# Weight sums of the first channel tile: from the vector engine to adding DMAs and a detour through DRAM

## The chip, the core and the metric

The kernel runs on one core of one Trainium2 chip. The metric is the device time of one execution in microseconds (us). A core has five engines that work side by side: TensorE (PE: matmuls, with weight loads as PEld), VectorE (DVE), ScalarE (ACT), GpSimd (POOL) and SyncE (SP, whose queue issues most DMAs here). Each works through its own list of instructions in order and waits on semaphores for the others.

## What is computed

One decoder layer with 1024 tokens, width 1024 and float32 data: a mixing sub-layer (attention heads and retention heads), an output projection, a layer norm, a GEGLU channel mixer with a causal convolution of width 3, a second layer norm.

```python
mix = jnp.concatenate([fox, ret], axis=-1) @ w_out[l]
x = layer_norm(ALPHA * x + g1 * mix, ln1_g[l], ln1_b[l])
h = x * (1.0 + sc2) + sh2
u = causal_depthwise_conv(h @ w_up[l], conv_w[l], conv_b[l])
a, bv = jnp.split(u, 2, axis=-1)
y = (jax.nn.gelu(a, approximate=False) * bv) @ w_down[l]
x = layer_norm(ALPHA * x + g2 * y, ln2_g[l], ln2_b[l])
```

The change lies in the weights of `h @ w_up`.

## The kernel before

**Stages.** Up to 224 us: retention and the input projections; then the values; 271 to 499: the attention heads, 8 heads of 8 query blocks each; about 476 to 579: the output projection, eight blocks of 128 tokens, each followed by its layer norm and its transposes; 579 to 1002: the up projection, 22 channel tiles of 128 (`NFF`); then the down projection.

**Three matmuls for one.** Every float32 operand is kept as two parts, a high part (rounded by ScalarE to the matmul's reduced format, `cast`) and a low part (VectorE, operand minus high part). A product is hi x hi + hi x lo + lo x hi: three matmuls.

**Seven products for eight.** For channel tile `ff` the kernel has two weight tiles of 128 x 1024, `a` (the GELU half) and `b` (the other half), each cut in two along the contraction: a0, a1, b0, b1, where a0 is `a[:, 0:4, :]`. With the tokens in two groups this is a 2 x 2 block product, done in Strassen's manner (Winograd's form) with seven products. Their weights are: 1: a0; 2: a1; 5: b0 + b1; 6: a0 + b0 + b1; 7: a0 + b0; 4: b1; 3: a1 + a0 + b0 + b1. The token operands are sums of the same kind, made by VectorE from the tiles `hr` and split into the pairs "11", "21", "22" and t1 to t4; product 7 takes t3, 4 takes t4, 3 takes "22".

**Who makes the weight sums.** `w_load` (L1185) brings a and b of a tile (512 KB each) from DRAM into R buffers. `w_a` splits a (products 1 and 2, tiles wA). `w_s` makes b0 + b1 and a0 + b0 + b1 on VectorE (L1209, L1211), then ScalarE casts the high part wS.h (L1191) and VectorE makes the low part wS.l (L1195). `w_d` adds a0 to b0 in place (L1224), and splits that with b1 (wD, products 7 and 4). `w_4` makes the sum for product 3 (L1232) and splits it (wZ, L1235 and L1236). For tile 0 this falls between the end of the output projection and product 7 of tile 0, where the last tokens' layer norm, transposes (`nT`, L898), activations (`hr`, L906) and operand splits (L875 on ScalarE, L879 on VectorE) also lie.

**Order on TensorE there.** `up_12(0)`: products 1 and 2 of tile 0; the last transposes; `up_65(0, 0)` and `up_12(1)`, mixed; the second halves of 6 and 5; then 7, 4 and 3 of tile 0; from then on 36 + 24 + 24 matmuls per tile.

**Buffers.** A tag names a ring of equal buffers: H 16, VM 10, R 4, X 16, S 3 (4 KB per partition each), T 4 (2 KB). A tile gets a buffer when the one in it has seen its last reader. At the end of the output projection the X buffers hold the eight `hr` tiles and the eight of the operands "11" and "21"; S holds the gate row and the rows `so` of the last blocks; R holds the mixed rows `mxs` of the output projection, then wa, wb and ws.

**The parking of w_out.** During the attention heads `w_out` is split ahead of its use: `park_load` brings a piece of 128 x 512 into a T buffer, `park_high` (L986) and `park_low` (L993) split it, `park_store` (L999) writes both parts to the DRAM tile `wod`; 16 pieces, one per three query blocks. `wo_load` (L1005) brings the parts back during the last head. In the same way `down_base` (L1105) copies parts of `w_down` from DRAM to DRAM (`td`, 256 KB each) and `add_to` (L1099) later adds to such parts with accumulating DMAs that GpSimd issues.

**What sets the order.** After the first part of the program, each engine's list is made by a planner: it takes the instruction that comes first in the source among those that it expects to be ready, so that loads often stand far ahead of their place in the source. `tc.issue_after(ins)` keeps what is traced in its block behind `ins`, on the engine of `ins` alone. `pins["nb"]` is the load (L749) of the bias row of the newest attention head.

Of the kernel before, what the change touches and what calls it, by code (L numbers as in the profile page):

```python
# [8 lines left out]
F32 = mybir.dt.float32  # L9
F32R = mybir.dt.float32r  # L10
# [5 lines left out]
P = 128  # L16
S = 1024
# [6 lines left out]
NFF = DFF // P  # L24
# [7 lines left out]
def kernel(  # L32
# [23 lines left out]
    nc = tc.nc  # L56
# [6 lines left out]
    dp = ctx.enter_context(tc.tile_pool(name="dp", bufs=1, space=bass.MemoryType.DRAM))  # L63
# [3 lines left out]
    def slot(tag, shape, dtype, name, padded=None):  # L67
        return gp.tile(shape, dtype, tag=tag, bufs=NB[tag], name=name, padded_shape=padded)

    def tmp(shape, dtype, name):  # L70
        return sp.tile(shape, dtype, tag="T", bufs=4, name=name, padded_shape=[P, 512])
# [4 lines left out]
    def f(ap):  # L76
# [14 lines left out]
        out=maskb, in_=maskb, pattern=[[-1, P]], compare_op=ALU.is_ge,  # L91
# [5 lines left out]
        out=tri, in_=tri, pattern=[[1, P]], compare_op=ALU.is_ge,  # L97
# [217 lines left out]
    for i in (0, 2):  # L315
        queued("DVE", nc.vector.tensor_scalar,
               out=bcol[:, i, :], in0=bcol[:, i, :], scalar1=1.0, scalar2=None, op0=ALU.add)
# [232 lines left out]
    for n in range(RH * NT):  # L550
        h, c = divmod(n, NT)
# [8 lines left out]
    for h in range(RH):  # L560
        t = max(2 * NT * (h + 1) + N0, ends[h] + 1)
# [41 lines left out]
    for m in range(NT - 1, RH * NT):  # L603
        h, c = divmod(m, NT)
# [118 lines left out]
    for q in range(2 * NT):  # L723
        n, c = 1 - q // NT, q % NT
# [19 lines left out]
    pins = {}  # L744
# [211 lines left out]
    def top_hi(key, c, sl):  # L956
        jp, n = TOPS[key]
        if key not in hop:
            op_tiles(key, "H")
        cols_hi(key, c, hr[jp + c, n], sl)  # L960

    def top_lo(key, c, sl):
        jp, n = TOPS[key]
        return cols_lo(key, c, hr[jp + c, n], sl)

    def h2_split(key, sl):
        for c in range(2):
            top_hi(key, c, sl)
            low = top_lo(key, c, sl)
        return low  # L970
# [1 line left out]


    wod = [dp.tile([2, P, D], F32, tag=f"wod{m}", name=f"wod{m}") for m in range(ND)]
    PIECES = [(m, slice(n, n + 512)) for m in (4, 5, 6, 7, 0, 1, 2, 3) for n in (0, 512)]
    park, wo = {}, {}

    def park_load(k):
        if k < len(PIECES):
            m, sl = PIECES[k]  # L980
            park[k] = [tmp([P, 512], F32, f"park{k}_{u}") for u in range(2)]
            nc.sync.dma_start(park[k][1], w_out[m * P:(m + 1) * P, sl])

    def park_high(k):
        hi, raw = park[k]
        nc.scalar.copy(hi.bitcast(F32R), raw)  # L986

    def park_low(k):

        if k in park:  # L990
            hi, raw = park[k]
            with tc.issue_after(pins["min"].ins):
                nc.vector.tensor_tensor(out=raw.bitcast(F32R), in0=raw, in1=hi, op=ALU.subtract)  # L993

    def park_store(k):
        if k in park:
            m, sl = PIECES[k]
            for u, t in enumerate(park.pop(k)):
                nc.sync.dma_start(wod[m][u][:, sl], t)  # L999

    def wo_load(m):
        wo[m] = []
# [50 lines left out]
    def op_mm(i, m4):  # L1053
        for n in range(2):
            op_half(i, m4, n)
# [29 lines left out]
    def op_end(i):  # L1085
        for n in range(2):
            op_sum(i, n)
        op_mean(i)
        op_norm(i)
# [8 lines left out]
    def add_to(dst, src):  # L1098
        return nc.gpsimd.dma_start(dst, src, accum_op=ALU.add, max_dma_last_dim=2048)  # L1099

    def down_base(m):
        for q, k in [divmod(v, NK) for v in range(m, 4 * NK, FH)]:
            t, n = ((0, 0), (1, 1), (1, 1), (1, 0))[q]
            with tc.issue_after(pins["nb"].ins):
                nc.sync.dma_start(td[q, k], wdq[t, k][:, n * 512:(n + 1) * 512])  # L1105

    LAG = 3
    LOADS = {0: (4, 5), 1: (6, 7), 2: (0, 1), 3: (2, 3)}
    T = {0: fox_alloc(0)}
# [5 lines left out]
    def proj(h, i):  # L1115
        if i < 3:
            fox_proj(h, w, T[h], 1, i + 1)
        elif h + 1 < FH:
            fox_proj(h + 1, w, T[h + 1], *divmod(i - 3, 4))

    for s_ in range(FH * NT + LAG + 1):
        h, i = divmod(s_, NT)
        if h < FH:
            if i == 0:
                if h % 4 == 0:
                    for half in range(2):
                        mixF[h // 4, half] = slot("VM", [P, 2, 512], F32, f"mixF{h // 4}_{half}")
            if i == 3:
                w = nw
                if h + 1 < FH:  # L1130
                    T[h + 1] = fox_alloc(h + 1)
            if i >= 3:
                proj(h, i)
            k, late = divmod(s_ - 4, 3)
            Sb[s_] = fox_scores(h, i, T[h], (lambda: park_low(k - 1)) if late == 1 else None)
            if i == 4 and h + 2 < FH:
                nw = fox_w(h + 2)
            if i == 6:
                down_base(h)
            if late == 0 and k >= 0:  # L1140
                park_load(k)
            if late == 1:
                park_store(k - 1)
            if late == 2 and k in park:
                with tc.issue_after(pins["exp"].ins):
                    park_high(k)
        r = s_ - LAG - 1
        if r >= 0 and r % 2 == 1:
            fox_pv(r // NT, (r % NT) // 2)
        r = s_ - LAG  # L1150
        if 0 <= r < FH * NT:
            fox_turn(r // NT, r % NT, Sb.pop(r))
        if h < FH and not (i >= 3):
            proj(h, i)
        if h == FH - 1 and i == 0:
            for q in range(2):
                op_load(q)
            g_row = slot("S", [P, D], F32, "g_row0")
            nc.sync.dma_start(g_row, bcast_rows(gates[0], D))
        if h == FH - 1:  # L1160
            for m in LOADS.get(i, ()):
                wo_load(m)
            if i in (2, 3):
                op_split(i - 2, 1)
            if i >= NT - 2:
                op_half(0, 1, i - NT + 2)
        if s_ == FH * NT:
            for q in range(2):
                x_load(q)
        if s_ == FH * NT + 1:  # L1170
            op_mm(1, 1)
            op_split(0, 0)
# [7 lines left out]
    ra, rb, rs, W = {}, {}, {}, {}  # L1180

    def w_load(ff, u):
        if ff < NFF:
            t = slot("R", [P, ND, P], F32, f"w{'ab'[u]}{ff}")
            nc.sync.dma_start(t, w_up[u * NFF + ff])  # L1185
            (ra, rb)[u][ff] = t
# [27 lines left out]
    def w_s(ff, tag="X"):  # L1214

        if ff < NFF:
            w_s_sums(ff)
            W[ff, 5], W[ff, 6] = w_split(rs[ff], tag, f"wS{ff}")

    def w_d(ff, tag="X"):  # L1220

        if ff < NFF:
            a, b = ra[ff], rb[ff]
            nc.vector.tensor_tensor(out=b[:, 0:4, :], in0=a[:, 0:4, :], in1=b[:, 0:4, :],  # L1224
                op=ALU.add)
            W[ff, 7], W[ff, 4] = w_split(b, tag, f"wD{ff}")

    def w_4(ff, tag="S"):

        if ff < NFF:  # L1230
            a, s = ra[ff], rs[ff]
            nc.vector.tensor_tensor(out=a[:, 4:8, :], in0=a[:, 4:8, :], in1=s[:, 4:8, :],  # L1232
                op=ALU.add)
            w = slot(tag, [P, 2, 4, P], F32R, f"wZ{ff}")
            nc.scalar.copy(w[:, 0], a[:, 4:8, :])  # L1235
            nc.vector.tensor_tensor(out=w[:, 1], in0=a[:, 4:8, :], in1=f(w[:, 0]),  # L1236
                op=ALU.subtract)
            W[ff, 3] = (w[:, 0], w[:, 1])
# [113 lines left out]


    for i in range(NT - 1):
        op_mm(i, 0)
        op_split(i + 1, 0)
        if i + 2 < NT:
            x_load(i + 2)
            op_load(i + 2)
            op_split(i + 2, 1)  # L1360
        op_end(i)
        if i > 0:
            h2_turn(i - 1)
            h2_low(i - 1)
            op_mm(i + 1, 1)

    w_load(0, 0)
    w_load(0, 1)
    w_load(1, 0)
    with tc.issue_after(pins["norm"].ins):  # L1370
        w_a(0, "VM")
# [10 lines left out]
    with tc.issue_after(pins["norm"].ins), tc.issue_after(pins["bias"].ins):  # L1382
        h2_split("t1", slice(0, 3 * P))
        up_12(0)
        w_s(0, "S")
        h2_turn(NT - 1)
        h2_low(NT - 1)
        for key in ("t2", "t1"):
            low = h2_split(key, slice(3 * P, 4 * P))
        up_65(0, 0)  # L1390
        with tc.issue_after(low.ins):
            up_12(1)
        w_d(0)
        h2_split("t3", slice(0, 4 * P))
        h2_split("t4", slice(0, 4 * P))
        w_4(0)
    w_load(1, 1)
    w_load(2, 0)

    for ff in range(NFF):  # L1400
        up_657(ff)
        w_s(ff + 1)
        w_d(ff + 1)
        w_load(ff + 2, 1)
        if ff + 2 == NFF:
            w_4(ff + 1)
        if ff > 0:
            up_12(ff + 1)
        if ff + 2 < NFF:
            w_a(ff + 2)  # L1410
        up_43(ff)
        if ff + 2 < NFF:
            w_4(ff + 1)
        w_load(ff + 3, 0)
        geglu(ff)
# [9 lines left out]
    late = []  # L1425
# [179 lines left out]
    for pi, p in enumerate(PORD[:-1]):  # L1605
# [5 lines left out]
        for k in range(NK):  # L1611
# [5 lines left out]
            else:  # L1617
                for i in range(4):
                    d_mm(p, k, i, pts[i], start and k == 0, stop and k == NK - 1)
                    if p == 7 and k == NK - 1:  # L1620
                        add = nc.vector.tensor_tensor(
                            out=s5[i], in0=s5[i], in1=X_[i], op=ALU.add)
# [105 lines left out]
```

## Time and profile before

| what | us |
|---|---|
| median of 3 runs (1222.0 to 1223.83) | 1222.03 |
| the profiled execution, whole | 1221.43 |
| its span, first to last instruction | 1219.7 |
| PE busy | 1200.4 |
| DVE busy | 908.9 |
| ACT busy | 652.6 |
| POOL busy | 226.7 |

The granted clock of TensorE was 0.998 of full speed on average. In the profile an engine's rows are instructions with a source line; the tile names carry no buffer numbers, so that `ws` stands for the sums of all 22 tiles. "Idle before, releaser" tells what ended an engine's wait. The chain of waits runs back from the last instruction to what released it, and shows which work set the time. DMA rows give the time from issue to landing.

### The profile page before, as it was taken

To read this page: it belongs to the slowest core of one execution; us is meant where nothing else is said; L and a number is where in the kernel's file an instruction comes from. 1 tells how busy PE (TensorE), PEld (TensorE's weight loads), DVE (VectorE), ACT (ScalarE), POOL (GpSimd) and SP (SyncE) were. 2 spreads that over 40 slices of the span, in tenths; PEclk is the share of its full clock that TensorE was granted. 3 is DMA by queue.
4 is the path that set the end of the run, shared out by engine and by line. 5 is a ranking of instruction groups with operands and counts; after the bars stand their busy time and mean duration, and the time that the engine had idled before them with its cause. 6 is when DMAs were issued, how large, how long until landed. Compare 5 with 4: busy or idle time off the path is not lost.

```text
span 1219.7 us, 17199 instructions
## 1 busy us (share of the span) xinstructions
PE 1200.4 (98%) x6005; PEld 1002.8 (82%) x6005; DVE 908.9 (75%) x1757; ACT 652.6 (54%) x1201; POOL 226.7 (19%) x274
## 2 busy tenths in 40 slices
PE   8999999999999999999999999999999999999997
PEld 6788888998888887888888888888888888888885
DVE  7857656766788888456988787787877886886586
ACT  6635434345777766567755445454454564543452
POOL 0015335012333333000012322211010010000021
PEclk9999999999999999999999999999999999999999
DMA  9524344614575559314259887786554588975751
GB/s 351 231 87 121 123 151 136 217 35 141 171 227 178 181 164 352 109 52 138 75 160 219 194 213 170 195 191 164 153 142 127 148 262 271 330 232 182 258 182 69
DMA packets 94279, 216.57 MB, mean 178 GB/s; under 512 B 10784, under 2 KB 17136, under 8 KB 94192
## 3 DMA queue, kind: packets, MB, share of 16 engines
q1 hardware_dynamic: 81520, 192.40, 46.0%
q0 software_dynamic: 12672, 23.07, 11.8%
q8 instruction: 47, 0.77, 0.3%
q14 instruction: 40, 0.33, 0.1%
HBM read 173.45 MB, written 76.59 MB: 205 GB/s over the span
## 4 chain that ended last, share of the span: by engine, by line
PE 86%; DMA 6%; DVE 4%; ACT 3%; issue 1%; SPq 0%; POOL 0%; DVEq 0%; ACTq 0%; POOLq 0%
PE rp L152 10%; PE dX L1469 10%; PE dZ L1469 7%; PE uX L1252 6%; PE uX L1251 6%; PE uX L1253 6%; PE uY L1251 5%; PE uY L1252 5%; PE uY L1253 5%; PE vp L152 4%; DMA ada<-in_ada_dram 3%; PE op L189 2%; PE op L191 2%; PE op L190 2%; PE pv L847 2%; PE qk L761 2%
## 5 line engine op out<-in xcount | busy, mean ns | idle before, releaser
L152 PE MATMUL rp<-wr,hhi 128*128 128x512 f32 x400 | 127.9, 401 | 0.0
L1458 DVE TENSOR_TENSOR dl<-dr,dh 128x1024 fp32r<-128x1024 f32 x66 | 80.2, 1237 | 35.6 <-ACT dh L1446 33.7
L1446 ACT CAST dh<-dr 128x1024 fp32r<-128x1024 f32 x66 | 68.0, 1050 | 72.3 <-DMA dr<-in_w_down_dram 32.9
L809 POOL TENSOR_TENSOR S<-S,dn 128x128 f32<-128x128 f32 (+3 forms) x64 | 73.2, 1148 | 156.9 <-DVE dn L808 132.7
L1099 POOL DMA_DIRECT2D sd<-gd x22 | 18.1, 823 | 397.6 <-DMA sd<-y 233.1
L152 PEld LDWEIGHTS rp<-wr,hhi 128*128 128x128 f32 x400 | 71.6, 189 | 12.7
L152 PE MATMUL rp<-wr,hlo 128*128 128x512 f32 x200 | 78.6, 393 | 0.0
L1469 PE MATMUL dX<-dl,dh 128*128 128x512 f32 x176 | 68.5, 389 | 0.0
L1469 PE MATMUL dX<-dh 128*128 128x512 f32 x176 | 68.5, 389 | 0.0
L1469 PE MATMUL dX<-dh,dl 128*128 128x512 f32 x176 | 68.5, 389 | 0.0
L1266 ACT COPY u<-uX 128x512 f32<-128x512 f32 x44 | 25.8, 585 | 69.7 <-PE uX L1253 69.7
L152 DVE CUSTOM_DVE_ANT_0 ada<-ada,csb,bcol 128x1024 f32<-128x1024 f32 x46 | 59.4, 1294 | 3.5 <-DMA ada<-in_ada_dram 3.5
L838 DVE TENSOR_TENSOR pt<-pt,pt 128x512 fp32r<-128x512 f32 (+2 forms) x96 | 50.7, 550 | 8.8 <-ACT pt L837 7.4
L805 ACT ACTIVATE S<-S,mn 128x128 f32<-128x128 f32 (+3 forms) x64 | 49.9, 780 | 13.4 <-DVE mn L798 13.0
L761 PE MATMUL qk<-hhi,wqh 128*128 128x512 f32 x128 | 55.1, 430 | 0.0
L798 DVE CUSTOM_DVE_ANT_0 S<-ps,nb 128x128 f32<-128x128 f32 (+3 forms) x64 | 47.4, 742 | 6.1 <-PE ps L796 5.9
L763 PE MATMUL qk<-hhi,wql 128*128 128x512 f32 x128 | 51.7, 404 | 0.0
L1469 PE MATMUL dZ<-dh 128*128 128x512 f32 x132 | 51.6, 391 | 0.0
L1469 PE MATMUL dZ<-dl,dh 128*128 128x512 f32 x132 | 51.4, 389 | 0.0
L1469 PE MATMUL dZ<-dh,dl 128*128 128x512 f32 x132 | 51.4, 389 | 0.0
L837 ACT CAST pt<-pt 128x512 fp32r<-128x512 f32 (+2 forms) x96 | 43.9, 479 | 13.6 <-PE pt L831 12.6
L189 PE MATMUL op<-wo,mxs 128*128 128x512 f32 x128 | 50.8, 397 | 0.0
(1046 smaller groups left out, 3652.2 us busy)
## 6 DMA issues: line engine op xcount, KB each, us to landing
ada<-in_ada_dram SPq DMA_DIRECT2D x48, 512.0 KB, 3.7
td<-in_w_down_dram SPq DMA_DIRECT2D x44, 256.0 KB, 6.0
wa<-in_w_up_dram SPq DMA_DIRECT2D x22, 512.0 KB, 4.7
wb<-in_w_up_dram SPq DMA_DIRECT2D x22, 512.0 KB, 4.3
gd<-y SPq DMA_DIRECT2D x22, 512.0 KB, 3.1
sd<-y SPq DMA_DIRECT2D x44, 256.0 KB, 3.3
dr<-sd SPq DMA_DIRECT2D x44, 256.0 KB, 3.8
dr<-td SPq DMA_DIRECT2D x44, 256.0 KB, 4.2
```

The lines of the kernel that those rows point to most:

```text
L152: order[key] = fn(*args, **kw)
L189: mm(pt, ahi, whi, start=start, stop=False)
L761: nc.tensor.matmul(pt, whi[:, j, :], hhi[j][:, sl], start=(j == 0), stop=False)
L763: nc.tensor.matmul(pt, wlo[:, j, :], hhi[j][:, sl], start=False, stop=(j == ND - 1))
L809: nc.gpsimd.tensor_tensor(out=Ssb[:, :span], in0=Ssb[:, :span], in1=den.to_broadcast([P, span]), op=ALU.mult,)
L838: nc.vector.tensor_tensor(out=dl, in0=src, in1=f(dh), op=ALU.subtract)
L1251: nc.tensor.matmul(pt, whi, bh, start=start, stop=False, skip_group_check=True)
L1252: nc.tensor.matmul(pt, whi, bl, start=False, stop=False, skip_group_check=True)
L1253: nc.tensor.matmul(pt, wlo, bh, start=False, stop=stop, skip_group_check=True)
L1446: nc.scalar.copy(hi, raw)
L1458: nc.vector.tensor_tensor(out=lo, in0=raw, in1=f(hi), op=ALU.subtract)
L1469: nc.tensor.matmul(pt, w_[:, 0, q], m_[:, 1, :], start=start and n_ == 0, stop=stop and n_ == 2, skip_group_check=True)
```

## The change

Tile 0's sums are made in DRAM. In head 6, block 2, SP issues four copies from DRAM to DRAM (`up_base`): b0, a0, a0 and a1 of tile 0 into `usum`. At the beginning of the output projection's loop GpSimd issues four adding DMAs (`up_adds`): b1 to the first, b0 to the third, then the first to the second, and the second to the fourth. That gives the weights of products 5, 6, 7 and 3; b1 itself is that of 4. These five blocks are appended to the pieces that are parked: in the loop over the output projection's blocks, `park_load` of one piece and the split and store of the one before it are added to blocks 0 to 5. In place of `w_s(0)`, `w_d(0)` and `w_4(0)` stand `up_parts` loads of the finished parts: two of 512 KB into S buffers (products 5 and 6), two of 512 KB into X buffers (7 and 4), two of 256 KB into S buffers (3). The load of b of tile 0 into an R buffer is gone. VectorE's part of `w_s(1)` is put behind the last split of t4.

```diff
-    PIECES = [(m, slice(n, n + 512)) for m in (4, 5, 6, 7, 0, 1, 2, 3) for n in (0, 512)]
+    PIECES = [(w_out[m * P:(m + 1) * P, n:n + 512], [wod[m][u][:, n:n + 512] for u in range(2)])
+              for m in (4, 5, 6, 7, 0, 1, 2, 3) for n in (0, 512)]
...
+    ua0, ub0 = [[w_up[u * NFF][:, k:k + 4, :] for k in (0, 4)] for u in range(2)]
+    usum = [dp.tile([P, 4, P], F32, tag=f"usum{k}", name=f"usum{k}") for k in range(4)]
+    upd = [dp.tile([P, 2 if k < 2 else 1, 4, P], F32, tag=f"upd{k}_{u}", name=f"upd{k}_{u}")
+           for k in range(3) for u in range(2)]
+    NW = len(PIECES)
+    flat = lambda t: t.rearrange("p k c -> p (k c)")
+    for n, src in ((3, ub0[1]), (0, usum[0]), (1, usum[1]), (2, usum[2]), (4, usum[3])):
+        PIECES.append((flat(src), [flat(upd[2 * (n // 2) + u][:, n % 2]) for u in range(2)]))
+
+    def up_base():
+        for k, src in ((0, ub0[0]), (1, ua0[0]), (2, ua0[0]), (3, ua0[1])):
+            with tc.issue_after(pins["nb"].ins):
+                nc.sync.dma_start(usum[k], src)
+
+    def up_adds():
+        for k, src in ((0, ub0[1]), (2, ub0[0]), (1, usum[0]), (3, usum[1])):
+            add_to(flat(usum[k]), flat(src))
+
+    def up_parts(n, tag, name):
+        out = []
+        for u, c in enumerate("hl"):
+            t = slot(tag, [P, 8 if n < 2 else 4, P], F32, f"{name}{c}")
+            nc.sync.dma_start(t, upd[2 * n + u].rearrange("p t k c -> p (t k) c"))
+            out.append(t.bitcast(F32R))
+        return [tuple(t[:, k:k + 4, :] for t in out) for k in ((0, 4) if n < 2 else (0,))]
...
+            if (h, i) == (6, 2):
+                up_base()
-            if late == 0 and k >= 0:
+            if late == 0 and 0 <= k < NW:
                 park_load(k)
...
     for i in range(NT - 1):
+        if i == 0:
+            up_adds()
+        park_load(NW + i)
         op_mm(i, 0)
...
         op_end(i)
+        if NW + i - 1 in park:
+            park_high(NW + i - 1)
+            park_low(NW + i - 1)
+            park_store(NW + i - 1)
...
     w_load(0, 0)
-    w_load(0, 1)
     w_load(1, 0)
...
         up_12(0)
-        w_s(0, "S")
+        W[0, 5], W[0, 6] = up_parts(0, "S", "wS0")
...
-        w_d(0)
+        W[0, 7], W[0, 4] = up_parts(1, "X", "wD0")
         h2_split("t3", slice(0, 4 * P))
-        h2_split("t4", slice(0, 4 * P))
-        w_4(0)
+        end = h2_split("t4", slice(0, 4 * P))
+        W[0, 3] = up_parts(2, "S", "wZ0")[0]
...
         up_657(ff)
-        w_s(ff + 1)
+        if ff == 0:
+            with tc.issue_after(end.ins):
+                w_s(ff + 1)
+        else:
+            w_s(ff + 1)
```

More of the change, by code (lines that the diff above doesn't have):

```diff
@@ L979, in park_load @@
         if k < len(PIECES):
-            m, sl = PIECES[k]
             park[k] = [tmp([P, 512], F32, f"park{k}_{u}") for u in range(2)]
-            nc.sync.dma_start(park[k][1], w_out[m * P:(m + 1) * P, sl])
+            nc.sync.dma_start(park[k][1], PIECES[k][0])
     def park_high(k):
@@ L996, in park_store @@
         if k in park:
-            m, sl = PIECES[k]
-            for u, t in enumerate(park.pop(k)):
-                nc.sync.dma_start(wod[m][u][:, sl], t)
+            for dst, t in zip(PIECES[k][1], park.pop(k)):
+                nc.sync.dma_start(dst, t)
     def wo_load(m):
```

## The prediction

> **What bounds the kernel now.** I read the page first, then the busy time in stretches of 20 us, then the chain of waits between 574 and 615 us, and then the timelines of the single engines there.
>
> ```profile
> PE 1200.4 (98%) x6005; PEld 1002.8 (82%) x6005; DVE 908.9 (75%) x1757; ACT 652.6 (54%) x1201; POOL 226.7 (19%) x274
> ```
>
> ```profile
> PE 86%; DMA 6%; DVE 4%; ACT 3%; issue 1%; SPq 0%; POOL 0%; DVEq 0%; ACTq 0%; POOLq 0%
> ```
>
> TensorE is the bound: it is busy for 98% of the span, and 86% of the chain that ended last is its own work. Work taken from another engine is worth only the TensorE idle time that it causes. So I look for that idle time. In these rows the columns are the stretch, its length, then the busy us of PE, PEld, DVE, ACT and POOL.
>
> ```profile
> 460.00:480.00 20.00, 18.24 (x111) 14.78 (x110) 16.46 (x49) 15.25 (x40) 7.46 (x7) 1.00 0.99 372
> 580.00:600.00 20.00, 19.10 (x110) 16.54 (x109) 19.77 (x37) 17.85 (x33) 0.00 (x0) 1.00 0.22 80
> 600.00:620.00 20.00, 20.00 (x89) 16.52 (x88) 19.86 (x23) 12.30 (x15) 0.00 (x0) 1.00 0.20 69
> ```
>
> The stretch 580 to 600, where the first channel tile's weights are summed and split, has VectorE full (19.77 of 20) and TensorE idle for 0.90 us. From 600 on TensorE is full again. The other gap that matters here is 1.76 us in 460 to 480. The chain (start, us, what) and TensorE's own timeline (start, duration, engine, line, operation, output<-inputs, and in brackets the idle time before it and its releaser) show the first:
>
> ```profile
> 594.67 0.96 ACT wD0h L1191
> 595.65 1.23 DVE wD0l L1195
> 596.87 1.15 DVE ht L879
> 598.07 0.50 PE uX L1252
> ```
>
> ```profile
> 596.70 0.46 PE L1251 MATMUL uX<-ht,wD0h 128*128 128x512 f32 x1
> 598.07 0.50 PE L1252 MATMUL uX<-ht,wD0h 128*128 128x512 f32 x1 [0.90 <-DVE ht L879]
> 606.17 0.39 PE L1251 MATMUL uX<-ht,wS1h 128*128 128x512 f32 x1
> 608.89 0.39 PE L1251 MATMUL uY<-ht,wS1h 128*128 128x512 f32 x1
> ```
>
> TensorE reaches product 7 (weights wD0) at 596.70 and stands before its second matmul, because VectorE wrote the low part of wD0 ahead of the low part of the token operand. From 606.17 to 608.89 twelve matmuls take 2.72 us. Products 7, 4 and 3 are 36 matmuls, so 8.16 us; from 596.70 to 606.17 they took 9.47. **The hole is 1.31 us, and that is all that the direct aim of the change can give.** I follow no other hole after it, since 600 to 620 has none.
>
> **The change part by part.** Removed in this stage are four sums, three low parts (VectorE) and three casts (ScalarE):
>
> ```profile
> 584.07 0.69 DVE L1209 TENSOR_TENSOR ws<-wb 128x512 f32<-128x512 f32 x1
> ...
> 586.00 0.69 DVE L1232 TENSOR_TENSOR wa<-wa,ws 128x512 f32<-128x512 f32 x1
> ...
> 588.07 1.21 DVE L1195 TENSOR_TENSOR wS0l<-ws,wS0h 128x1024 fp32r<-128x1024 f32 x1
> ...
> 593.50 1.42 DVE L879 TENSOR_TENSOR ht<-hr,ht 128x256 fp32r<-128x256 f32 x4
> ...
> 599.06 0.69 DVE L1236 TENSOR_TENSOR wZ<-wa,wZ 128x512 fp32r<-128x512 f32 x1
> ```
>
> ```profile
> 586.54 1.05 ACT L1191 CAST wS0h<-ws 128x1024 fp32r<-128x1024 f32 x1
> ```
>
> ```profile
> 588.22 2.90 ACT L906 ACTIVATE hr<-nT,AB 128x128 f32<-128x128 f32 x8
> ```
>
> VectorE loses 4 x 0.69 + 1.21 + 1.23 + 0.69 = 5.9 us, ScalarE 1.05 + 0.96 = 2.0 us and the smaller cast of wZ. With wD0l gone the token operand that stopped TensorE is ready at least 1.2 us earlier, so the old hole closes: **-1.31**. VectorE was late, not early, in 600 to 620, so what it gains there keeps TensorE fed and the shift should last to the end.
>
> *wD0 now comes by DMA, and that is the new wait.* It needs two X buffers. All 16 are taken at that point: eight hold hr, eight hold the operands 11 and 21 that live on. So the two loads of 512 KB can't start before hr buffers are given back, which happens as the four pieces of the row at 593.50 end: the first two at about 593.9 and 594.2. How much earlier does that come? VectorE would be 2.5 + 1.2 = 3.7 us ahead, but the pieces follow the eight activations at 588.22, which only wS0h (1.05 us) held back. I take 1.0: release at 592.9 and 593.2. The prices of such loads (the last column is the us from issue to landing), alone at 589 and as a pair that was issued 1.1 us apart:
>
> ```profile
> wb<-in_w_up_dram SPq DMA_DIRECT2D x1, 512.0 KB, 3.5
> ```
>
> ```profile
> 606.32 0.33 SPq L1185 DMA_DIRECT2D wb<-in_w_up_dram  x1
> 607.45 0.33 SPq L1185 DMA_DIRECT2D wa<-in_w_up_dram  x1
> ```
>
> ```profile
> wb<-in_w_up_dram SPq DMA_DIRECT2D x1, 512.0 KB, 4.7
> wa<-in_w_up_dram SPq DMA_DIRECT2D x1, 512.0 KB, 4.8
> ```
>
> TensorE wants the high part at 596.70 and the low part two matmuls later, at 597.15. By the pair's price they land at 597.6 and 598.0: a new stall of 0.9. By the lone price they land at 596.4 and 596.7: none. Without the 1.0 of advance and at the pair's price the low part lands at 599.0: 1.85. The pair is the nearer row, since the two are issued almost together, but part of the products needs no low part; I take **+0.6** (0 to 1.85). [...] No row here has two such loads released together, so the trace leaves it open.
>
> *wS0 and wZ0.* The S tag has three buffers: the rows of the gate, so of block 6 and so of block 7 hold them before. Two come free by the last gate product at 580, so wS0's two loads land by 584 against a first use at 588; I cost them at nothing. Their cover is that SP issues them ahead of the last x1d store, on which it stood until 585.8:
>
> ```profile
> 574.14 11.64 SPq L1083 DMA_DIRECT2D x1d<-acc  x2
> ```
>
> Behind it they would land at 589.3 or later, and the 24 matmuls of the second tile's products 1 and 2 (5.4 us), which TensorE ran in that stretch before, would fill that. wZ0 is two tiles now, so the stage asks for four S buffers: the last load waits until wS0h has been read, at 596.70. At 3.5 us it lands at 600.2; product 3, if last of the three, starts at 602.1. Nothing again. wb of tile 0 is not loaded and ws of tile 0 is not made, so R buffers come free earlier and the weights of tiles 1 and 2 arrive sooner.
>
> *The five new pieces.* The same work was done 16 times before (ns: least, median, most):
>
> ```profile
> L986 ACT CAST park<-park x16: 603/607/632, 298.9 to 446.7; 128x512 fp32r<-128x512 f32 x16
> L993 DVE TENSOR_TENSOR park<-park,park x16: 678/689/1166, 302.4 to 451.1; 128x512 fp32r<-128x512 f32 x16
> ```
>
> ```profile
> 499.00:546.00 47.00, 47.00 (x225) 39.01 (x224) 23.07 (x63) 29.65 (x70) 0.00 (x0) 1.00 0.22 78
> ```
>
> Five times 0.61 is 3.0 us of ScalarE and five times 0.69 is 3.4 us of VectorE, in a stretch where they are idle for 17 and 24 us and TensorE never waits: 0. Were that cover gone, a split of the mixed rows would come 1.3 us late per piece. The adds run on POOL, which has nothing to do there. An add of 256 KB landed in 5.8 us, and three follow on each other, 17.4 us, with some 70 us of room; SP would stand behind a late one, and the x and so loads with it.
>
> ```profile
> sd<-gd POOLq DMA_DIRECT2D x1, 256.0 KB, 5.8
> ```
>
> *The four base copies and the early loads* fall into the attention stage, where DMA ends on the chain:
>
> ```profile
> 413.65 6.69 DMA wqkr<-in_w_qk_dram
> ```
>
> ```profile
> 458.82 6.16 DMA so<-mixR
> ```
>
> ```profile
> 415.36 2.76 SPq L1105 DMA_DIRECT2D td<-in_w_down_dram  x4
> 418.91 0.33 SPq L749 DMA_DIRECT2D nb<-cum_d  x1
> ```
>
> ```profile
> 459.81 13.13 SPq L1005 DMA_DIRECT2D wo<-wod  x13
> ```
>
> ```profile
> 466.71 0.63 PE L831 MATMUL pt<-ident,S 128*128 128x128 f32 x4 [1.16 <-DVE mixF L854]
> ```
>
> The base copies hang on the nb load of head 6 alone, so the planner will issue them as it did those of td: behind the four of head 5, after wqkr. SP spends 2.76 / 4 = 0.69 us on one, 2.8 in all, and nb of head 7 goes behind them; it is first read some 40 us later. 13 wo loads took 13.13 us, so 256 KB cost 0.5 us of transfer, the four copies 2.0; what they push back is a piece's load and the cast that ScalarE has lined up for it. **+0.1** (0 to 2.0): added traffic can't hurry anything. The first new piece is raw weight and needs no add; T has four buffers, so up to two new loads can slip in ahead of so at 458.82, for which ScalarE stood, and then TensorE at 466.71: **+0.3** (0 to 1.0).
>
> Sum: -1.31 + 0.6 + 0.1 + 0.3 = -0.3. The profiled execution took 1221.43 us (span 1219.7 and 1.7 around it), so 1221.1 there; the median of the runs is 1222.03, 0.60 above it, and I carry the difference over: **1221.7 us**. The ends of the terms give -1.3 to +3.5, though they will hardly fall together.
>
> **The rivals.**
> *The hole closes for good.* If the two loads don't slow each other (3.5 us each), nothing replaces the stall and the attention stage doesn't notice: -1.3, so 1220.7. For it: DMA is busy for 0.22 of 580 to 600. Against it: the pair at 606.
> *wD0 arrives late.* SP works in order. If its loads stand in SP's queue behind the last wZ0 load, which can't go before 596.70, they land at 596.7 + 4.8 = 601.5, and TensorE waits from 597.15: 4.35 in place of 1.31, so +3.0, with the 0.4 of the attention stage 1225.5. It makes the kernel slower as soon as the low part lands after 598.1, and measurably so after about 600.5. For it: VectorE, ScalarE, X buffers and SP all have to be right within 4 us, where before only two engines had to. Against it: the source asks for wD0 before wZ0.
> *More falls than the hole.* A new order from 412 us on also removes most of the 1.16 us hole at 466.71: with the first rival -2.5, 1219.5. Only luck speaks for it.
> *The change doesn't do what it says.* The sums may not be what held VectorE: the token operand waits for ScalarE instead and the hole stays, at +0.4: 1222.4. The chain speaks against it, since wD0h and wD0l stand in it themselves.
>
> **How the numbers follow.** A measurement of this kernel can tell about 0.2%, 2.4 us, from no change. Forecast 0.55, first rival 0.18, late wD0 0.19, more falls 0.06, no effect 0.02. Late wD0 counts as slower, more falls as faster, the rest as the same: faster 0.06, same 0.75, slower 0.19. The range runs from the third rival's time to the second's, 1219.5 to 1225.5; the forecast's own range, where the same-sized cases lie, is 1220.6 to 1223.5.
>
> **What would show it.** In the changed profile: no sums, casts or low parts of tile 0 between 584 and 600; VectorE under 19 of 20 us in that stretch; wD0's loads issued about 593 on SP; the matmuls of product 7 either without a gap (first rival) or with one below 1 us that ends on a DMA (forecast); the hole at 466.71 no larger than 2.2 us; TensorE without idle time from 480 to 590. The prediction is wrong if product 7 waits over 2.5 us, if TensorE idles in the output projection behind a split, or if wqkr of head 7 lands later than 6.7 us after its issue.

## The result, and the profile after

The changed kernel takes 1231.95 us (median of six runs, 1230.53 to 1233.97); the kernel before, run beside it, takes 1222.59 (six runs). The difference of the two medians is 9.4 us. The ratio on record is 1.0082, with a 95% interval of 1.0072 to 1.0092 (the quotient of the medians is 1.0077): slower. One execution of a later kernel, `late_add`, had a granted clock of 0.556 and took 2011.92 us; the times and ratios below leave it out. The profiled execution took 1231.91 us, its span 1230.2, against 1219.7 before. The forecast was 1221.7, and no rival had this loss.

Two lines of the page after, the busy times of the engines and the shares of the chain that ended last:

```profile
PE 1203.7 (98%) x6005; PEld 1004.5 (82%) x6005; DVE 907.3 (74%) x1755; ACT 653.2 (53%) x1203; POOL 229.7 (19%) x278
PE 83%; DMA 7%; ACT 4%; DVE 4%; issue 1%; SPq 0%; POOL 0%; DVEq 0%; ACTq 0%; POOLq 0%
```

TensorE is as much the bound as it was, with the same 6005 matmuls; nothing on the page names a culprit. The busy time by stretches does (stretch, length, busy us of PE, PEld, DVE, ACT, POOL, then the granted clock). First the changed kernel:

```profile
440.00:460.00 20.00, 14.11 (x72) 12.05 (x73) 9.09 (x24) 7.16 (x17) 6.72 (x7) 0.83 0.55 163
460.00:480.00 20.00, 17.37 (x108) 14.11 (x107) 14.14 (x42) 14.04 (x34) 6.84 (x6) 1.00 0.84 304
480.00:500.00 20.00, 19.39 (x117) 15.74 (x115) 17.09 (x44) 11.69 (x28) 7.33 (x5) 1.00 0.84 314
500.00:520.00 20.00, 19.65 (x100) 16.35 (x98) 12.79 (x30) 10.70 (x21) 0.00 (x0) 1.00 0.73 227
580.00:600.00 20.00, 20.00 (x107) 16.93 (x107) 14.84 (x34) 17.55 (x37) 0.00 (x0) 1.00 0.49 172
600.00:620.00 20.00, 19.83 (x100) 16.41 (x100) 19.47 (x30) 14.66 (x23) 0.00 (x0) 1.00 0.35 119
1000.00:1020.00 20.00, 18.94 (x83) 14.96 (x82) 17.71 (x16) 11.95 (x14) 1.62 (x2) 1.00 0.82 242
```

Then the two stretches of the kernel before that the prediction did not show and that answer to these:

```profile
440.00:460.00 20.00, 19.88 (x120) 16.69 (x120) 15.96 (x41) 13.16 (x28) 5.45 (x4) 1.00 0.34 114
980.00:1000.00 20.00, 19.61 (x87) 15.93 (x86) 17.40 (x17) 13.22 (x15) 2.48 (x3) 1.00 0.93 261
```

The transition, at which the change aims, is what was forecast: TensorE idle for 0.17 us between 580 and 620, against 0.90. The loss lies 140 us earlier. Between 440 and 460 TensorE is idle for 20 - 14.11 = 5.89 us, against 0.12, and runs at a lower clock. TensorE's own timeline has the place (start, duration, line, operation, in brackets the idle time before it and its releaser):

```profile
445.89 1.12 PE L831 MATMUL pt<-ident,S 128*128 128x128 f32 x4 [6.01 <-POOL S L809]
```

It is the attention stage: the transposes of a block of scores wait for POOL, which scales the scores at line 809. POOL's timeline tells what it did:

```profile
425.27 0.98 POOL L1098 DMA_DIRECT2D usum<-in_w_up_dram  x1
428.26 0.82 POOL L1098 DMA_DIRECT2D usum<-in_w_up_dram  x1
434.07 0.81 POOL L1098 DMA_DIRECT2D usum<-usum  x1 [4.99 <-DVE mn L798]
434.62 1.98 POOL L809 TENSOR_TENSOR S<-S,dn 128x896 f32<-128x896 f32 x1
443.10 0.82 POOL L1098 DMA_DIRECT2D usum<-usum  x1 [6.51 <-DMA usum<-usum]
443.67 3.87 POOL L809 TENSOR_TENSOR S<-S,dn 128x1024 f32<-128x1024 f32 x4
```

The four adds (line 1098) stand in the attention stage, not in the output projection where the source has them: nothing but the four base copies holds them, so the planner moved them up. The third adds the first's result, the fourth the third's. For the fourth, POOL stands still for 6.51 us until the third has landed, and behind it in POOL's list stand the scalings, four of which then run without a pause; TensorE is waiting for the first. The third add had waited too, 4.99 us: the first, issued at 425.27, landed after 8.5 us. (The bracket names an instruction of VectorE that ended just after that; in `adds_only` below the same wait, 5.65 us there, is put down to the first add.) That wait cost TensorE next to nothing: it idles for 0.50 us from 420 to 440, against 0.44 before. The wait is an order of instructions, not work: POOL is busy for 6.72 of those 20 us.

The clock makes it worse. The wait, and the stretch behind it (the clock is the number after POOL's):

```profile
440.00:445.90 5.90, 0.01 (x1) 0.01 (x1) 1.05 (x3) 0.10 (x1) 2.80 (x4) 0.86 1.04 330
445.90:451.20 5.30, 5.30 (x17) 4.46 (x18) 2.80 (x6) 2.86 (x5) 1.63 (x3) 0.52 0.61 148
```

TensorE is full again from 445.9, but at 0.52 of its clock for 5.3 us, which costs 5.3 x 0.48 = 2.5 us more. The clock falls to 0.50 at 444.2, 4.3 us after TensorE went idle, and is back at 1.00 from about 451.0; in the kernel before, which has no such wait, it is 1.00 over the whole stretch from 440 to 460. The traces show that the two go together, not what couples them.

So the 10.5 us of span are: 5.8 of idle time at 440 to 460, 2.5 of clock, 1.5 between 460 and 500 (2.63 + 0.61 against 1.76 before; profiles without any early piece differ by up to 0.8 there, see `parks_late`), -0.7 at the transition, +0.7 at the end of the up projection (1.06 against 0.39 from 980 to 1020); the 0.7 that are left lie mostly between 500 and 540.

The chain of waits of the changed kernel gives the wrong name here (start, us, what):

```profile
438.59 5.04 DMA td<-in_w_down_dram
443.67 2.18 POOL S L809
445.89 1.12 PE pt L831 x4
```

It follows POOL back to a DMA, a copy of td. No instruction of POOL's there needs td; in its list, the fourth add waits for the landing of the third. The timeline's bracket has it right.

### The profile page after: what moved, and what is told of

Read it like the earlier page. It is cut to its first block, busy times and chain, and to the rows that moved or that the text cites. A ratio compares the mean times of both kernels' runs of the same rounds, so it can differ in the third digit from the quotient of the medians.

```text
span 1230.2 us, 17270 instructions
## 1 busy us (share of the span) xinstructions
PE 1203.7 (98%) x6005; PEld 1004.5 (82%) x6005; DVE 907.3 (74%) x1755; ACT 653.2 (53%) x1203; POOL 229.7 (19%) x278
## 4 chain that ended last, share of the span: by engine, by line
PE 83%; DMA 7%; ACT 4%; DVE 4%; issue 1%; SPq 0%; POOL 0%; DVEq 0%; ACTq 0%; POOLq 0%
PE rp L152 10%; PE dX L1507 10%; PE dZ L1507 7%; PE uX L1279 6%; PE uX L1281 6%; PE uX L1280 6%; PE uY L1281 5%; PE uY L1279 5%; PE uY L1280 5%; PE vp L152 4%; DMA ada<-in_ada_dram 3%; PE pv L847 2%; PE op L191 2%; PE op L189 2%; PE op L190 2%; PE qk L761 2%
## 5 line engine op out<-in xcount | busy, mean ns | idle before, releaser
L831 PE MATMUL pt<-ident,S 128*128 128x128 f32 x288 | 47.0, 279 | 9.1 <-POOL S L809 6.0
L762 PE MATMUL qk<-hlo,wqh 128*128 128x512 f32 x128 | 51.4, 402 | 0.0
```

Of the source, the lines that this page charges most:

```text
L762: nc.tensor.matmul(pt, whi[:, j, :], hlo[j][:, sl], start=False, stop=False)
```

## Experiments

**The adds alone, with and without the wait between them.** Two kernels put the four base copies and the four adds into the kernel before, where nothing reads the result: `adds_only` with the change's code, and `adds_free`, in which the last two adds take their source from the weights, so that no add waits for another. These two, and `copies_only`, `no_adds` and `pin_two` below, were run once each, with the profiler; the kernel before took 1219.95 to 1223.49 us in the runs beside them.

```diff
 def up_adds():
-    for k, src in ((0, ub0[1]), (2, ub0[0]), (1, usum[0]), (3, usum[1])):
+    for k, src in ((0, ub0[1]), (2, ub0[0]), (1, ub0[1]), (3, ub0[0])):
         add_to(flat(usum[k]), flat(src))
```

> The kernel before with the base copies and the four adds alone, at the change's places; nothing reads their result, and all weights of tile 0 are summed on VectorE as before. Theory A: the whole of the main loss appears without any of the rest: a gap of about 6 us near 440 with half the clock after it, 1230 to 1231 us. Theory C: 1222 to 1223.

> The kernel before with the four base copies and four adds, whose result nothing reads; the third and fourth add take their source from the weights and not from a sum, so they wait for no other add. Bytes, places on POOL and sources in DRAM are those of adds_only (1228.6, gap 6.85 us at 446). Theory (POOL stands on the landing of an earlier add, and the scaling queued behind it stands with it): no gap over 1 us between 438 and 452, 1221.5 to 1223.0. Rival (DMA traffic or the issue of adds on POOL): the gap of 6 us stays, 1227 to 1229.

`adds_only` took 1228.59 us, span 1226.9, so 7.2 us of span over the kernel before: less than the 1230 to 1231 expected, so the adds alone make the large part of the 10.5 us and not all. TensorE has the same gap:

```profile
445.95 1.12 PE L831 MATMUL pt<-ident,S 128*128 128x128 f32 x4 [6.85 <-POOL S L809]
```

`adds_free` took 1221.92 us, span 1220.2. Its POOL timeline, and the stretch of the gap:

```profile
425.49 1.84 POOL L1099 DMA_DIRECT2D usum<-in_w_up_dram  x2 [0.58 <-DMA usum<-in_w_up_dram]
428.18 2.29 POOL L1099 DMA_DIRECT2D usum<-in_w_up_dram  x2
434.06 2.25 POOL L809 TENSOR_TENSOR S<-S,dn 128x1024 f32<-128x1024 f32 x2 [1.88 <-PE pt L831]
```

```profile
440.00:460.00 20.00, 19.87 (x120) 16.77 (x120) 15.57 (x42) 13.43 (x29) 6.03 (x5) 1.00 0.66 230
```

Four adds of as many bytes in the same stage, the last two issued from 428.18 on since they wait for no other add: no gap. Traffic and the issue of adds on POOL are not the cause; the wait of one add for another is (for the fourth add 6.51 us in the changed kernel, 6.71 in `adds_only`), with the scalings queued behind it.

**The copies alone** (`copies_only`: the kernel before and `up_base`), **and the change without its adds** (`no_adds`: no call of `up_adds`, so the weights of products 5, 6, 7 and 3 of the first channel tile are left unsummed).

> The kernel before with the four base copies alone (no add, nothing reads them). Theory: 1 MB of copies is hidden but for what it pushes back: 1221.4 to 1222.6, the waits at 440 to 480 no larger than before by more than 0.5 us. Rival (the added traffic of 418 to 440 us delays so or the parked pieces): 1223.5 to 1225, with a gap before 480 that ends on a DMA or on ScalarE behind one.

> The changed kernel without the four adds: products 5, 6, 7 and 3 of tile 0 take unsummed weights. Copies, five pieces and six loads stay. Theory A: no gap near 440, 1222 to 1224 us. Theory B with the copies as the cause: 1227 or more.

`copies_only` took 1220.56 us, span 1218.9, below the expected range: the 1 MB of copies is hidden. `no_adds` took 1224.32, span 1222.6, just above its range. It has no gap at 446, but a longer wait at 467 (1.16 us in the kernel before) and a lower clock behind it:

```profile
466.92 0.63 PE L831 MATMUL pt<-ident,S 128*128 128x128 f32 x4 [1.86 <-DVE mixF L854]
```

```profile
466.90:471.00 4.10, 4.08 (x17) 3.14 (x18) 3.45 (x10) 3.70 (x10) 0.83 (x1) 0.61 1.02 416
```

The clock of 0.61 costs 1.6 us there. From 980 to 1020 it loses 1.39 + 0.16 = 1.55 us. So it says that the adds are the large part of the loss, and not that the rest is free.

**The adds later.** In `pin_adds` all four stand behind the last scaling in POOL's list, in `pin_two` only the two that wait:

```diff
-        nc.gpsimd.tensor_tensor(
+        pins["mul"] = nc.gpsimd.tensor_tensor(
...
+            with tc.issue_after(pins["mul"].ins):
-            add_to(flat(usum[k]), flat(src))
+                add_to(flat(usum[k]), flat(src))
```

> The changed kernel with one edit: the four adding DMAs are put behind the last softmax scaling (L809) on GpSimd's list. Theory A (GpSimd's queue: the fourth add stands at 443.10 for the third to land, 6.51 us, the scaling of block 7 stands behind it, TensorE idles 6.01 us and then runs 5.3 us at a granted clock of 0.52): the gap at 445.9 is gone, 8.2 to 8.6 us come back, 1223.3 to 1223.8 us, or 1.001 of before; what is left over is the second-order loss around 490 to 520. Theory B (the added traffic of four copies and four adds, DMA busy 1.00 of 420 to 440): the copies still run there, so TensorE still loses several us around 440 and the time stays over 1227. Theory C (the loss is in the new loads of the up projection): no change, 1232.

> As the changed kernel, but only the two adds that read the result of another add are put behind the last softmax scaling; the two first adds stay in the attention stage, each behind a base copy. Theory A: it is the wait for another add, not the issue of an add, that costs: no gap over 1.5 us in 420 to 460, time as with all four moved, 1223 to 1225. If the issue of an add on GpSimd or its traffic is what counts, about half of the loss stays: 1226 to 1229.

`pin_adds` closed the gap at 446 and yet took 1230.22 us (ratio 1.0068, 1.0054 to 1.0082): a miss. POOL, ScalarE and TensorE of this kernel:

```profile
498.89 0.81 POOL L1098 DMA_DIRECT2D usum<-usum  x1 [7.52 <-DMA usum<-usum]
```

```profile
501.42 0.62 ACT L986 CAST park<-park 128x512 fp32r<-128x512 f32 x1 [6.14 <-DMA upd<-park]
506.86 0.62 ACT L986 CAST park<-park 128x512 fp32r<-128x512 f32 x1 [4.44 <-DMA upd<-park]
```

```profile
515.03 1.97 PE L898 MATMUL nT<-ident,acc 128*128 128x128 f32 x8 [5.17 <-ACT acc L1081]
```

The same fault one engine further: POOL's wait (7.52 us) now holds up nobody. But the casts of the new pieces, which the planner had lined up early in ScalarE's list, stand there for 6.14 and 4.44 us with the first block's norm behind them, for which TensorE waits 5.17 us (the granted clock is 0.84 over 500 to 520). What ends both waits is, by the brackets, the landing of a store of an earlier piece (`upd<-park`): a piece takes two of the four T buffers, so a cast has to wait until an earlier piece has left them. The first wait is for one of the two stores issued from 491.67 on:

```profile
upd<-park SPq DMA_DIRECT2D x2, 256.0 KB, 9.7
```

The sums of the two waiting pieces had been loaded by then: the loads were issued at 490.30 and 498.63 and landed after 7.6 and 4.4 us, 3.5 and 3.8 us before the casts ran. So the late sums are a part of the wait, and the longer part is for buffers. `pin_two`, whose first two sums are ready early, took 1225.26 us, with a small remainder of that wait, and loses 2.88 us between 980 and 1020:

```profile
510.71 1.09 PE L898 MATMUL nT<-ident,acc 128*128 128x128 f32 x8 [1.17 <-ACT acc L1081]
```

**The pieces later.** `parks_late` leaves the adds where the change has them and moves the five pieces: each is loaded behind the x1d store of the block before (its normed rows, to DRAM), and cast and split behind that block's norm. `pin_all` has this and `pin_adds`.

```diff
-        park_load(NW + i)
+        if i > 0:
+            with tc.issue_after(pins["x1d"].ins):
+                park_load(NW + i - 1)
...
         if NW + i - 1 in park:
-            park_high(NW + i - 1)
-            park_low(NW + i - 1)
+            with tc.issue_after(pins["norm"].ins), tc.issue_after(pins["bias"].ins):
+                park_high(NW + i - 1)
+                park_low(NW + i - 1)
             park_store(NW + i - 1)
```

> The change with the adds where the planner put them, but the five pieces moved as in pin_all. Theory (the POOL wait costs about 8 us and the pieces' cast about 1.5 to 2): the gap of about 6 us at 446 with the slower clock behind it stays, the wait of ScalarE on pieces at 505 to 515 is gone: 1229.3 to 1230.8, so 1.2 to 2.6 under the changed kernel's 1231.95. Rival (the pieces cost nothing in the changed kernel; all is POOL's): 1231.5 to 1232.5.

> The whole change, with both of the new waits moved: the four adds stand on POOL behind the last scaling of the attention stage, and each new piece is loaded behind the store of the previous block's x1d on SP, with its cast behind that block's norm on ScalarE and its low part behind that block's bias on VectorE. Theory (the loss is two in-order waits, first POOL's on the landing of an add, then ScalarE's on a piece that is not ready): no gap at 446, none at the nT transposes of the first block (about 510 us), products 7 of the first channel tile with at most 0.3 us: 0.9 to 1.3 under the kernel before, so 1220.7 to 1221.5, ratio 0.9989 to 0.9996, unless the end of the up projection loses up to 1 us as in the other runs (then up to 1222.5). Rival (the added transfers themselves cost, wherever the adds stand): still 1226 or more. Second rival (the wait moves on again, to SP behind a late load of a piece or to TensorE at the loads of wS0): 1223.5 or more, with a new gap of over 1 us that ends on a DMA between 500 and 600 us.

`parks_late` took 1231.01 us, ratio 1.0074 (1.0061 to 1.0088), which the changed kernel's interval overlaps: the time doesn't tell the two apart, and it lies between the ranges of the theory and the rival. In its profile TensorE does not idle at all from 500 to 540 (0.35 + 0.14 us in the changed kernel): that share of the pieces is gone. From 460 to 500 it idles for 1.45 + 0.42 us (2.63 + 0.61 in the changed kernel, 1.76 in the one before). That this is the pieces' too is not shown: the same stretch has 1.98 and 2.60 us in the two profiles of `pin_all` and 2.46 us in `pool_sums`, which adds no DMA (all below).

But the third add landed later there, and the gap at 446 is longer:

```profile
446.51 1.11 PE L831 MATMUL pt<-ident,S 128*128 128x128 f32 x4 [7.33 <-POOL S L809]
```

`pin_all` took 1221.82 us, ratio 1.0000 (0.9991 to 1.0009). Against `pin_adds`, the late pieces are worth 8 us; against `parks_late`, the late adds 9. The rows of its stretches:

```profile
440.00:460.00 20.00, 19.88 (x122) 16.63 (x119) 15.63 (x41) 13.16 (x29) 5.71 (x5) 1.00 0.42 149
500.00:520.00 20.00, 20.00 (x98) 16.50 (x97) 9.64 (x28) 13.01 (x28) 0.00 (x0) 1.00 0.46 161
580.00:600.00 20.00, 19.94 (x114) 17.20 (x113) 17.18 (x31) 15.27 (x29) 0.00 (x0) 1.00 0.37 132
980.00:1000.00 20.00, 17.42 (x76) 13.78 (x74) 14.52 (x14) 11.99 (x14) 2.36 (x3) 1.00 0.76 212
1000.00:1020.00 20.00, 19.58 (x86) 16.24 (x87) 15.00 (x14) 8.80 (x9) 1.62 (x2) 1.00 0.79 256
```

Both waits are gone, the hole of the transition is closed, and this profiled execution still took 1225.1 us: it loses 2.58 + 0.42 = 3.0 us between 980 and 1020, where the kernel before loses 0.39.

**Is the gain given back there?** `pin_all_again` is the same kernel, profiled a second time; `pool_sums` closes the hole in another way, without any DMA: the kernel before with two of the first tile's four sums on POOL.

```diff
-            nc.vector.tensor_tensor(out=b[:, 0:4, :], in0=a[:, 0:4, :], in1=b[:, 0:4, :],
+            (nc.vector if ff else nc.gpsimd).tensor_tensor(out=b[:, 0:4, :], in0=a[:, 0:4, :], in1=b[:, 0:4, :],
...
-            nc.vector.tensor_tensor(out=a[:, 4:8, :], in0=a[:, 4:8, :], in1=s[:, 4:8, :],
+            (nc.vector if ff else nc.gpsimd).tensor_tensor(out=a[:, 4:8, :], in0=a[:, 4:8, :], in1=s[:, 4:8, :],
```

> The same kernel as pin_all, on the chip beside pool_sums, for a second profile and a narrower interval. Theory (the changed stages gain 1.1 us by 970 us, and the 3.0 us that its first profile lost between 980 and 1020 are loads that landed late in that execution): ratio 0.9990 to 1.0000, and a loss between 980 and 1020 that differs from 3.0 us by more than 0.5. Rival (the loss at the end of the up projection belongs to this kernel): again 2.5 to 3.5 us there.

> The kernel before, without any added DMA, with two of the four sums of the first channel tile (the one that becomes wD0 and the one that becomes wZ0) made on POOL in place of VectorE: VectorE has 2 x 0.69 = 1.38 us less between 584 and 600. Theory (the hole at product 7 is VectorE being about 1.2 us late, and closing it is worth what it was, whatever way it is closed): the 0.90 us wait at product 7 falls to 0.3 or less, 580 to 600 us has TensorE idle for at most 0.3, and the time is 0.6 to 1.0 us under the kernel before, ratio 0.9992 to 0.9995, which five rounds can hardly tell from 1. Rival (ScalarE, with wD0h and the token operands, is as late as VectorE): the wait stays at 0.6 or more and the time is that of before. Second rival (what is gained at 600 is given back at the end of the up projection, where casts wait for loads of the down projection): wait closed, but TensorE idle for more than 1 us between 980 and 1020, against 0.39 in the kernel before.

`pin_all_again`: 1223.21 us, ratio 1.0002 (0.9991 to 1.0012). Its stretches at the end of the up projection:

```profile
980.00:1000.00 20.00, 17.73 (x77) 14.01 (x76) 14.37 (x14) 12.28 (x14) 2.44 (x3) 1.00 0.78 216
1000.00:1020.00 20.00, 19.14 (x84) 15.88 (x85) 15.44 (x15) 8.76 (x9) 1.05 (x2) 1.00 0.77 249
```

Again 2.27 + 0.86 = 3.1 us: that loss belongs to this kernel as it is profiled, against what I expected. `pool_sums`: 1222.9 us, ratio 1.0006 (0.9997 to 1.0015). Its hole did not close, as its first rival had it; it split:

```profile
591.40 0.39 PE L1253 MATMUL uX<-ht,wS0l 128*128 128x256 f32 x1 [0.31 <-DVE wS0l L1195]
598.96 0.50 PE L1252 MATMUL uX<-ht,wD0h 128*128 128x512 f32 x1 [0.65 <-DVE ht L879]
```

VectorE's own timeline, while POOL makes the two sums (585.77 to 589.40), shows where the room went:

```profile
586.99 1.25 DVE L879 TENSOR_TENSOR ht<-hr,ht 128x768 fp32r<-128x768 f32 x1 [0.71 <-ACT ht L875]
588.76 1.45 DVE L879 TENSOR_TENSOR ht<-hr,ht 128x768 fp32r<-128x768 f32 x1
```

The two sums that were taken away are worth 1.4 us. Beside POOL's sums these two splits took 1.25 and 1.45 us, for 0.95 each in the kernel before, and VectorE stood 0.71 us for ScalarE. So this run says nothing on whether a gain at 600 is kept.

What differs at 980 is an order. There the rows y of the channel mixer are stored to DRAM (gd) and added up (sd) for the down projection, whose operands are loaded as dr. In the kernel before, SP's load of dr and then POOL's add that takes a half of gd, each from its engine's timeline:

```profile
981.49 0.43 SPq L1438 DMA_DIRECT2D dr<-in_w_down_dram  x1
```

```profile
981.55 0.81 POOL L1099 DMA_DIRECT2D sd<-gd  x1 [17.14 <-DMA gd<-y]
```

The same two in `pin_all`, the add first:

```profile
979.92 0.81 POOL L1098 DMA_DIRECT2D sd<-gd  x1 [16.98 <-DMA gd<-y]
```

```profile
980.38 0.43 SPq L1480 DMA_DIRECT2D dr<-in_w_down_dram  x1
```

Counted from the store of gd (976.82 and 975.71) the add comes after 4.73 us before, behind the pair of loads, and after 4.21 in `pin_all`, ahead of it; there the load issued at 980.38 lands after 9.3 us. The profiles of the kernels with the change's loads have the add at 4.15 to 4.25 and lose 0.6 to 3.1 us in this stretch, those without have it at 4.6 to 4.9 and lose 0.4 to 0.7. `late_add` tests whether this is the cause:

```diff
+                if ff == 19 and m == 2:
+                    nc.gpsimd.dma_start(idle, gd[ff, 0:1, 512:1024])
                 after = add_to(d, e)
```

> pin_all with one more small DMA on POOL (2 KB, read from gd of channel tile 19, written to a scratch that nothing reads), issued between the landing of that gd store and the add of sd<-gd that follows it at 980 us. In both profiles of pin_all this add was issued 4.2 us after the gd store, just ahead of a pair of dr loads, and TensorE lost 3.0 and 3.1 us between 980 and 1020; in the profiles of the kernels without the change's loads it was issued 4.6 to 4.9 us after the store, behind that pair, and the loss was 0.4 to 0.65. The extra DMA delays the add by about 0.8 us. Theory (the place of the add among the dr loads decides how late the last of these lands): the add goes behind the pair, the loss between 980 and 1020 falls to 0.3 to 1.0, and the time is 2 to 2.7 us under that of pin_all, 1219.3 to 1220.3, ratio 0.9975 to 0.9990. Rival (the early add is a sign and not the cause): the loss stays at 2.5 to 3.5 and the ratio is 0.9995 to 1.0010.

In its profiled execution (1220.51 us, span 1218.8) the small DMA and the add stand so on POOL, the add at the same time as the pair's second load (979.85) and not behind it, and this is the row of that stretch:

```profile
979.34 0.52 POOL L1379 DMA_DIRECT2D idle<-gd  x1 [16.85 <-DMA gd<-y]
979.85 0.86 POOL L1098 DMA_DIRECT2D sd<-gd  x1
```

```profile
980.00:1000.00 20.00, 19.47 (x86) 15.61 (x85) 17.43 (x17) 11.81 (x13) 2.31 (x3) 1.00 0.86 259
```

The loss falls from 3.0 to 0.53 in this one profile, as expected. The time doesn't follow: 1221.8 us, ratio 1.0002 (0.9991 to 1.0012), as for `pin_all`. Either the executions without the profiler do not lose there what the profiled ones lose, or the scatter (single runs of either kernel lie 4 to 5 us apart) hides it. That stays open, and with it what moves the add by half a microsecond.

## Why the prediction was wrong

**The step that failed** is in the part on the pieces: "The adds run on POOL, which has nothing to do there." It took the place in the source for the place in the queue. For SP's copies I asked where the planner would put them, and said: in the attention stage. I did not ask it for the adds, which hang on these copies alone. There POOL scales every block of scores, and the view of SP's queue was read where POOL's was needed. The price that I had for an add, 5.8 us to land, would have been enough: two of the four adds wait for another one, and one such wait with the scalings behind it (6.51 us on POOL) stopped TensorE for 6.01. The chain itself had been seen ("three follow on each other, 17.4 us"), but it was held against the time left until the sums are used, and not against what stands behind it on POOL. So the adds entered the sum as nothing, where they cost 5.8 us of idle time and 2.5 of clock. The list of queues that the prediction goes through has SP's and ScalarE's, and not POOL's.

**The size of an add.** 5.8 us was the price of an add alone. In the attention stage of the changed kernel, where DMA was busy for 1.00 of the time from 420 to 440, these landed later (last column):

```profile
usum<-in_w_up_dram POOLq DMA_DIRECT2D x2, 256.0 KB, 8.1
usum<-usum POOLq DMA_DIRECT2D x2, 256.0 KB, 7.9
```

**The five new pieces, at 0,** were right for the room on ScalarE and VectorE and wrong for their order: a cast that waits, here for a buffer that an earlier piece has not left, holds up what is queued behind it (in `pin_adds` two casts waited 6.14 and 4.44 us, and the first block's norm behind them, on a ScalarE that is busy for 11.63 of the 20 us from 500 to 520). In the changed kernel this is a part of 2 us at most; in `pin_adds` it was nearly the whole loss. I had named the price of a late split ("1.3 us late per piece") as work and not as a wait.

**The base copies (+0.1, 0 to 2.0)** were about right: `copies_only` took 1220.56 us, though TensorE idles 0.6 us more from 460 to 480. **The early loads (+0.3, 0 to 1.0)** can't be judged: 460 to 500 lost 1.5 us more in the changed kernel than before, and 0.1 with the pieces moved, but 0.2 and 0.8 in two profiles of one kernel and 0.7 in `pool_sums`, which has no such loads.

**The transition (-1.31, +0.6)** came out as forecast in sum: from the first matmul of the first tile (579.00 before, 589.27 after) to the first with wS1 (606.17 and 615.69) it takes 0.75 us less, for -0.71. That the two terms met this sum is partly luck: what is left of the hole is mainly another wait than the forecast one. The two loads of wD0 in SP's queue:

```profile
603.28 0.32 SPq L1129 DMA_DIRECT2D wD0h<-upd  x1
603.70 0.38 SPq L1129 DMA_DIRECT2D wD0l<-upd  x1
```

TensorE begins the first tile 10.27 us later than before; less that, the loads are issued at 593.0 and 593.4, for a forecast of 592.9 and 593.2, and the second lands after 4.6 us, near the pair's price of 4.7 to 4.8. The new stall on it is small, since the planner put two matmuls of product 3 between, which needed neither: one weight load waits 0.3 us for wD0l. TensorE's own wait is the one that the fourth rival named, for ScalarE's part of the token operand:

```profile
607.15 0.47 PE L1279 MATMUL uX<-ht,wD0h 128*128 128x512 f32 x1 [0.17 <-ACT ht L875]
```

Of the three conditions under which I called the prediction wrong, one came true in part (TensorE waits 0.49 us in the output projection for a norm that has pieces before it) and the decisive one was missing: a wait of the scores for POOL.

## What to carry to other kernels

Before costing an instruction that is added to a queue, find out where in that queue it will stand: if a planner orders the work, it stands as early as its inputs allow, not where the source has it (here the four adds, at 425 to 443 us). Then list what is behind it, and take its wait, not its work, as the price; here POOL, busy for 19% of the span, stopped TensorE for 6.01 us because its next instruction waited. When such a wait is moved, look at once for the next consumer that has been lined up early, since the wait can move on to it (here from POOL, 6.51 us, to ScalarE, 6.14 and 4.44 us in `pin_adds`).

## What the hardware showed beside that

A gap of TensorE of 5.17 to 7.33 us was each time followed by half the clock: for 5.1 us in the changed kernel (gap 6.01 us, so that this wait cost 8.5), for 3.7 us in `adds_only` (6.85), for about 6 in `parks_late` (7.33), and in `pin_adds` (5.17, to 515.03) for the rest of the stretch up to 520 at least. Shorter gaps in the same place (466 to 476 us) went both ways: 1.86 us (`no_adds`) and 2.46 us (`pool_sums`) were followed, about 1 us later, by 3.4 to 3.8 us at half the clock (a mean of 0.91 over 460 to 480 in both), while 1.67, 2.00 and 2.10 us (`adds_free`, `pin_all_again`, the changed kernel) were not (1.00 over 460 to 480 in all three). With the part that lies in the gap itself, the clock stood at half for 6.8 us in all in the changed kernel (444.2 to 451.0); the means of the stretches give 6.6 to 7.0 us in `adds_only` (0.83 over 440 to 460), at least 6.2 in `pin_adds` (0.84 over 500 to 520) and 10.2 to 10.6 in `parks_late` (0.74 over 440 to 460). In the six profiles in which it fell in these stretches that is about once, twice or three times 3.4 us, the half of the 6.8. What a wait cost here is therefore not proportional to its length, and near 2 us it changed from profile to profile (each kernel named here has one).
